# Expert 0 and the emptiest expert in turns, the plan between halves of a chunk, and the gate's bias from columns on chip

## The chip, the cores and the metric

The kernel runs on one core of a Trainium2 chip. The metric is the time of one execution on the device in microseconds (us); a profile shows one execution with every instruction of the engines: TensorE (PE), VectorE (DVE), ScalarE (ACT), GpSimd (POOL) and SyncE (SP, which here only issues transfers).

## What is computed

Two residual layers on 256 tokens of width 1024, all float32. Layer 0 is a mixer (gated delta rule beside a state-space model) and a dense SwiGLU. Layer 1 is differential attention and a mixture of experts. Before each part stands an RMS norm whose scale, shift and output gate come from `cond @ ada_w + ada_b`:

```python
mod = cond @ ada_w[layer] + ada_b[layer]          # 6 x 1024: sh1, sc1, g1, sh2, sc2, g2
x = x + g1 * mixer_or_attention(rmsnorm(x) * (1 + sc1) + sh1)
h = rmsnorm(x) * (1 + sc2) + sh2
logits = h @ router_w                             # 8 experts; the two largest of each token
for e in range(8):
    out += combine[:, e] * ((silu(h @ w1[e]) * (h @ w3[e])) @ w2[e])
x = x + g2 * out
```

The experts' weights are 8 x 33 MiB: w1 and w3 of 1024 x 2816 each, w2 of 2816 x 1024.

## The kernel before

**Weights and the ring.** Weights come from memory in tiles of 128 partitions, 1 MiB each (0.75 MiB for the third chunk), by `raw` (L105) and in `up` (L1742), all issued from SP in one queue, in order. In the expert stage there are 12 such tiles, used in a ring: a load goes out when the last use of the load twelve before it is over.

**Two forms of an expert.** Expert 0 and those with many tokens are large (128 places): `up_big` (L1656) and `down_big` split each weight tile into a rounded part `whi` (ACT, L131) and a rest `wlo` (DVE, L132) and make three products (L1674 to L1676, L1707 to L1709). The others are small (64 places): `up` (L1712 on, products L1731, L1737) and `down` (L1782) use the float32 tiles directly, in four column groups of PE. The up projection is cut into three chunks of the 2816 columns (1024, 1024, 768). Each chunk of `up_big` has two halves: first all products with w1, then a Silu, then all products with w3, then the product of both and transposes (`pth`). `tail` is a function that is called in the middle of a chunk: there the scatter of the expert before is put.

**Places and order.** `gather(r)` (L1607) brings the tokens of one expert into a buffer `xg` by products with a 0/1 matrix `Pt`; `scatter` (L1786) adds the results to `x`, with buffers `yf`, `yh`, `yl`. `plan()` (L1445) counts tokens, ranks experts 1 to 7 by count, writes the ranks' expert numbers (`idi`, L1475), their places and weights (`posS`, `combS`), and reads the numbers into registers of SP (`self.who`), which give the addresses of all weights but expert 0's; it returns `way`, which chooses among four arms of code by how many experts are large. `WAYS` gives for each the order of the ranks; rank 7 is the emptiest. In the profiled data ranks 1 and 2 are large: the order is 7, 1, 6, 5, 2, 4, 3.

Before the arms, the code runs in this order: gather 0, chunk 0 of expert 0, plan, chunks 1 and 2, gather 7, the down projection of expert 0, then the up projection of rank 7 with expert 0's scatter in its first chunk. Down of rank 7 and all else follow in the arm. The order of instructions on each engine is made by a scheduler from the order of the program and its own estimates, so that later work can stand between parts of earlier work.

**The gate's bias.** `ada_end` (L285) ends one of 24 column groups of a layer's `mod`: a sum over partitions by a product with ones. For the output gates (`which` 2 and 5, four groups each in each layer, 16 calls) it loads 256 values of `ada_b` by SP (L295), adds them to one row on POOL (L296), and makes a product that spreads the sum to all partitions (L297), which ACT copies (L298). `colA` (L231) holds all of `ada_b` on chip from the start, transposed: column 48 l + 2 j + b holds 128 values. Two of the 16 calls stand in the expert stage's beginning, four in the dense layer, the others in the mixer and the attention.

Of the kernel before, what the change touches and what calls it, by code (L numbers as in the profile page):

```python
# [9 lines left out]
F32 = mybir.dt.float32  # L10
F32R = mybir.dt.float32r
I32 = mybir.dt.int32
AF = mybir.ActivationFunctionType
ALU = mybir.AluOpType
# [3 lines left out]
P = 128  # L18
T = 256
NT = 2  # L20
D = 1024
KD = 8
# [4 lines left out]
NE = 8  # L27
# [47 lines left out]
class Trunk:  # L75
# [209 lines left out]
    def ada_end(self, l, j, s, who):  # L285
        self.mark(f"ada{l}_{j}")
        nc = self.nc
        which, o = j // 4, j % 4
        pb = self.ps(self.adatag, "gvb")
        if which in (2, 5):  # L290
            key = (l, which // 3)
            if key not in self.gates:
                self.gates[key] = (self.cp if key == (1, 1) else self.scr).tile([P, D], F32, name=self.nm("gate"), tag="gate", bufs=1)
            b = self.scr.tile([1, 256], F32, tag="adab", name=self.nm("adab"), bufs=1)
            nc.sync.dma_start(b, self.a["ada_b"][l:l + 1, 256 * j:256 * j + 256])  # L295
            nc.gpsimd.tensor_tensor(s[0:1, :], s[0:1, :], b, op=ALU.add)  # L296
            nc.tensor.matmul(pb[:, :256], who.to_broadcast([P, P]), s, start=True, stop=True)  # L297
            nc.scalar.activation(self.gates[key][:, 256 * o:256 * o + 256], pb[:, :256], AF.Copy)  # L298
            return
        for b in range(2):  # L300
            pe = nc.tensor.matmul(pb[:, b:b + 1], s[:, b * P:(b + 1) * P], who, start=True, stop=True)
        col = self.modc[(l, which)][:, 2 * o:2 * o + 2]
        b0 = l * 48 + j * 2
        nc.vector.tensor_tensor(col, pb[:, :2], self.colA[:, b0:b0 + 2], op=ALU.add)
        if which in (1, 4):
            w0 = (96 if which == 1 else 112) + l * 8 + 2 * o
            dve = nc.vector.scalar_tensor_tensor(col, col, 1.0, self.colA[:, w0:w0 + 2], op0=ALU.add, op1=ALU.mult)
            self.lastada = [pe.ins, dve.ins]
# [1089 lines left out]
    def moe(self):  # L1398
        self.mark("moe")
        nc, a, mp = self.nc, self.a, self.mp  # L1400
# [5 lines left out]
        def t(name, shape=SH):  # L1406
            return mp.tile(list(shape), F32, name=name)
# [14 lines left out]
        m1, m2, r = (t(x, (P, NT)) for x in ("m1", "m2", "r"))  # L1422
# [76 lines left out]

        self.big, self.posS, self.combS, self.who = NE, pos, comb, [0]  # L1500
        xg = self.gather(0)
        hs = []
        for c in range(len(self.CHUNKS)):
            with self.behind(self.lasts if c < 1 else ()):
                self.up_big(0, c, xg[0], hs, None)
            if c == 0:
                way = plan()
        self.big, r = 1 + self.SPLITS[-1], NE - 1
        xg1 = self.gather(r, "Pt1")
        py, steps = self.down_big(0, hs, 0, D)  # L1510
        for step in steps:
            step()
        tail, hs = partial(self.scatter, 0, py, self.places(0, xg[1]), 0, D), []
        for c in range(len(self.CHUNKS)):
            self.up(r, c, xg1[0], hs, tail if c == 0 else None, "h1")
        tc, begun, at = self.tc, (hs, xg1[1]), self.nraw

        def arm(n):
            if n + 1 == len(self.SPLITS):
                self.arm(n, begun, at)  # L1520

                with tc.If(way > n):
                    for m, caps in enumerate(self.CAPS[1:]):
                        for r in range(NE):
                            V.tensor_scalar(self.posS[:, :, r], self.posS[:, :, r], -float(self.CAPS[m][r]), None, op0=ALU.add)
                        self.experts([r for r in (0,) + self.WAYS[n] if caps[r]])
                return
# [6 lines left out]
    def arm(self, n, begun, at):  # L1534
        self.nraw, self.nsplit = at, 0
        self.big = 1 + self.SPLITS[n]
        self.experts(self.WAYS[n], begun)

    SPLITS = (2, 3, 4)
    WAYS = ((7, 1, 6, 5, 2, 4, 3), (7, 1, 6, 2, 5, 3, 4), (7, 1, 2, 6, 3, 4, 5))

# [58 lines left out]
    def mtile(self, name, shape, bufs=1, dt=F32):  # L1604
        return self.mp.tile(list(shape), dt, tag=name, name=self.nm(name), bufs=bufs)

    def gather(self, r, own="Pt"):  # L1607

        self.mark(f"gather{r}")
        V, S, PE, tile = self.nc.vector, self.nc.scalar, self.nc.tensor, self.mtile  # L1610
        big = r < self.big
        n = P if big else 64
        Pt = tile(own, (P, NT, n if own != "Pt" else P), 2 if own == "Pt" else 1)
        for tt in range(NT):
            ins = V.tensor_scalar(Pt[:, tt, :n], self.c("iota")[:, :n], self.posS[:, tt, r:r + 1], None, op0=ALU.is_equal).ins
        self.lasts = [self.xTlast, ins]
        xg = tile("xg", (P, KD, 2, P), 1, F32R)
        if not big:
            xg = xg.bitcast(F32)[:, :, 0, :]
        for k0 in range(0, KD, 4):  # L1620
            px = self.ps("ms", "px")
            for kk in range(4):
                k = k0 + kk
                for tt in range(NT):
                    PE.matmul(px[:, kk * n:kk * n + n], self.xn[:, tt, k * P:(k + 1) * P], Pt[:, tt, :n], start=(tt == 0), stop=(tt == 1))  # L1625
            f = tile("yf", (P, 512)).rearrange("p (k s) -> p k s", s=P) if big else xg[:, k0:k0 + 4]
            for kk in range(4):
                k = k0 + kk
                S.activation(f[:, kk, :n], px[:, kk * n:kk * n + n], AF.Identity, bias=self.shc[:, k:k + 1], scale=self.scc[:, k:k + 1])
            if big:  # L1630
                ks = slice(k0, k0 + 4)
                V.tensor_copy(xg[:, ks, 0, :], f)  # L1632
                V.tensor_tensor(xg[:, ks, 1, :], f, xg[:, ks, 0, :], op=ALU.subtract)
        return xg, Pt
# [202 lines left out]
```

## Time and profile before

| | us |
|---|---|
| median of 3 runs | 1382.24 (1381.57 to 1384.51) |
| profiled execution | 1378.09 |
| its span, first to last instruction | 1376.3 |
| PE busy | 1281.9 (93%) |
| DVE busy | 826.4 (60%) |
| ACT busy | 577.1 (42%) |
| transfers | 400.98 MB, mean 291 GB/s |

Busy time is that in which an engine works on an instruction; matmuls are pipelined, so a busy PE need not be at its peak. The granted clock of PE is 0.978 of full speed in the mean. Lines as L132 are lines of the kernel before; a line can be that of a helper, and `x88` counts instructions. A float32 product is two instructions.

### The profile page before, as it was taken

The numbers are of one execution on the slowest core, as the hardware profiler recorded it, in microseconds if no ns is written. First come the engines' busy times: TensorE is split into PE (matmuls) and PEld (weight loads), VectorE is DVE, ScalarE is ACT, GpSimd is POOL, SyncE is SP. The second block draws the span as 40 slices with busy tenths as digits, with TensorE's granted clock in tenths as the row PEclk, the third lists the DMA queues.
The fourth block names the chain that finished last, engine by engine and source line by source line (L and its number), as shares of the span: only waits on it lengthen the run. The fifth ranks groups of instructions, "written<-read, shape, count | busy, mean of one in ns | idle before, by whom it ended". The sixth has DMA issues, their size and how long they took to land.

```text
span 1376.3 us, 26749 instructions
## 1 busy us (share of the span) xinstructions
PE 1281.9 (93%) x10928; PEld 941.8 (68%) x10928; DVE 826.4 (60%) x1516; ACT 577.1 (42%) x990; POOL 123.6 (9%) x118
## 2 busy tenths in 40 slices
PE   3999999989999978999999999999998899999975
PEld 2777666779999978998788435786352468835334
DVE  6688767567878878965798413986020089820202
ACT  3553322455444444664778213775010168711000
POOL 3132322000000003341100000000000000000000
PEclk9799999999999999999999999999999999999998
DMA  9834334159788967821899899999999999999995
GB/s 262 268 114 132 111 106 154 62 177 325 247 270 287 293 211 252 271 96 63 334 305 399 305 380 409 405 409 356 391 409 405 408 409 406 409 397 408 408 396 208
DMA packets 196164, 400.98 MB, mean 291 GB/s; under 512 B 14797, under 2 KB 115650, under 8 KB 196034
## 3 DMA queue, kind: packets, MB, share of 16 engines
q1 hardware_dynamic: 189610, 398.00, 78.7%
q10 hardware_dynamic: 6424, 1.19, 0.5%
q8 instruction: 88, 1.44, 0.4%
q14 instruction: 42, 0.34, 0.1%
HBM read 398.11 MB, written 1.05 MB: 290 GB/s over the span
## 4 chain that ended last, share of the span: by engine, by line
PE 46%; DMA 10%; DVE 4%; issue 1%; ACT 1%; SPq 1%; POOL 0%; ACTq 0%; DVEq 0%
PE pab L1731 9%; DMA raw<-in_odd_expert_w 9%; PE py L1782 5%; PE pab L1675 4%; PE pab L1674 4%; PE pab L1676 4%; PE py L1708 2%; PE py L1709 2%; PE py L1707 2%; PE px L1625 2%; DVE wlo L132 1%; PE pqk L398 1%; PE pqk L399 1%; PE pqk L400 1%; PE pth L150 1%
## 5 line engine op out<-in xcount | busy, mean ns | idle before, releaser
L131 ACT ACTIVATE whi<-raw 128x1024 fp32r<-128x1024 f32 (+2 forms) x352 | 347.1, 1001 | 279.8 <-PE pab L399 52.3
L132 DVE TENSOR_TENSOR wlo<-raw,whi 128x1024 fp32r<-128x1024 f32 (+2 forms) x352 | 402.9, 1168 | 72.6 <-ACT whi L131 70.6
L1731 PE MATMUL pab<-raw,xg 128*32 128x512 f32 (+1 forms) x1920 | 194.2, 524 | 10.5 <-DMA raw<-in_odd_expert_w 10.5
L1731 PEld LDWEIGHTS pab<-raw,xg 128*32 128x32 f32 x1920 | 58.2, 109 | 118.8 <-issue 77.5
L1751 DVE TENSOR_TENSOR hb<-hb,pab 128x256 f32<-128x256 f32 (+1 forms) x35 | 12.4, 364 | 171.0 <-ACT hb L1750 170.5
L1675 PE MATMUL pab<-wlo,xg 128*128 128x512 f32 (+1 forms) x288 | 110.3, 383 | 3.6 <-DVE wlo L132 3.4
L1676 PE MATMUL pab<-whi,xg 128*128 128x512 f32 (+1 forms) x288 | 106.4, 377 | 0.0
L398 PE MATMUL pab<-hT,whi 128*128 128x256 f32 x352 | 101.9, 290 | 0.0
L399 PE MATMUL pab<-hT,whi 128*128 128x256 f32 x352 | 100.3, 285 | 0.1
L400 PE MATMUL pab<-hT,wlo 128*128 128x256 f32 x352 | 99.9, 284 | 0.0
L1782 PE MATMUL py<-raw,hTe 128*32 128x256 f32 (+1 forms) x1760 | 83.7, 343 | 10.7 <-DMA raw<-in_odd_expert_w 8.6
L282 DVE SCALAR_TENSOR_TENSOR adas<-raw,condr,adas 128x256 f32<-128x256 f32 x175 | 86.4, 499 | 3.1
L1674 PE MATMUL pab<-whi,xg 128*128 128x512 f32 (+1 forms) x288 | 84.4, 379 | 3.6 <-DVE xg L1632 1.9
L1782 PEld LDWEIGHTS py<-raw,hTe 128*32 128x32 f32 x1760 | 53.4, 112 | 38.0 <-DMA raw<-in_odd_expert_w 12.8
L1802 DVE TENSOR_TENSOR yf<-py,gate 32x256 f32<-32x256 f32 (+1 forms) x48 | 18.0, 374 | 102.3 <-PE py L1782 101.3
L1750 ACT ACTIVATE hb<-pab 128x256 f32<-128x256 f32 (+1 forms) x35 | 11.5, 338 | 155.8 <-PE pab L1731 155.1
L399 PEld LDWEIGHTS pab<-hT,whi 128*128 128x128 f32 x352 | 68.0, 193 | 0.8 <-DVE hT L388 0.5
L398 PEld LDWEIGHTS pab<-hT,whi 128*128 128x128 f32 x352 | 68.1, 193 | 0.3
L400 PEld LDWEIGHTS pab<-hT,wlo 128*128 128x128 f32 x352 | 67.9, 193 | 0.1
L1675 PEld LDWEIGHTS pab<-wlo,xg 128*128 128x128 f32 x288 | 54.3, 189 | 19.4 <-DVE wlo L132 6.3
L1676 PEld LDWEIGHTS pab<-whi,xg 128*128 128x128 f32 x288 | 54.4, 189 | 10.0
L1674 PEld LDWEIGHTS pab<-whi,xg 128*128 128x128 f32 x288 | 51.0, 189 | 13.7 <-ACT whi L131 2.2
(465 smaller groups left out, 2504.4 us busy)
## 6 DMA issues: line engine op xcount, KB each, us to landing
raw<-in_odd_expert_w SPq DMA_DIRECT2D x215, 1024.0 KB
raw<-in_ada_w SPq DMA_DIRECT2D x48, 1024.0 KB
raw<-in_odd_expert_w SPq DMA_DIRECT2D x64, 768.0 KB
raw<-in_even_ffn_w SPq DMA_DIRECT2D x33, 1024.0 KB
raw<-in_odd_w_qkv SPq DMA_DIRECT2D x12, 1024.0 KB
raw<-in_even_w_in SPq DMA_DIRECT2D x10, 1024.0 KB
raw<-in_even_w_out SPq DMA_DIRECT2D x4, 1024.0 KB
raw<-in_odd_w_out SPq DMA_DIRECT2D x4, 1024.0 KB
```

The source lines that it names most:

```text
L131: act = nc.scalar.activation(hs, src, AF.Copy)
L132: dve = nc.vector.tensor_tensor(l, src, hs, op=ALU.subtract)
L282: nc.vector.scalar_tensor_tensor(s, w[:, k, :], self.condr[:, k, 0:1], s, op0=ALU.mult, op1=ALU.add)
L398: nc.tensor.matmul(out, wh[:, o:o + P], hT[:, k, 0, :], start=(k == 0), stop=False)
L399: nc.tensor.matmul(out, wh[:, o:o + P], hT[:, k, 1, :], start=False, stop=False)
L400: nc.tensor.matmul(out, wl[:, o:o + P], hT[:, k, 0, :], start=False, stop=(k == kd - 1))
L1625: PE.matmul(px[:, kk * n:kk * n + n], self.xn[:, tt, k * P:(k + 1) * P], Pt[:, tt, :n], start=(tt == 0), stop=(tt == 1))
L1674: PE.matmul(p[:, :m], xg[:, k, 0, :], wh[:, s], start=(k == 0), stop=False)
L1675: PE.matmul(p[:, :m], xg[:, k, 0, :], wl[:, s], start=False, stop=False)
L1676: PE.matmul(p[:, :m], xg[:, k, 1, :], wh[:, s], start=False, stop=(k == KD - 1))
L1731: PE.matmul(pu[t][32 * g:32 * g + 32], xg[:, k, 32 * t:32 * t + 32], v[:, :, g * n:(g + 1) * n], start=(k == 0 and (t == 0 or n > P)), sto ...
L1782: PE.matmul(py[32 * g:32 * g + 32, t], hs[f][t], v[:, i, g * n:(g + 1) * n], start=(f == 0 and t == 0), stop=(f == NF - 1 and t == 1))
```

## The change

Four edits. The bias of the gate is added by two more products into the same accumulator, a column of `colA` spread over 128 columns against the identity; the load, the small buffer and the POOL addition go. The plan is called as `tail` of expert 0's first chunk, between its two halves. The up projection of rank 7 stands between the chunks of expert 0: expert 0 chunk 0, chunk 1, gather 7 (its output in the buffer `yh` instead of `xg`), rank 7 chunk 0, expert 0 chunk 2, rank 7 chunk 1, expert 0 down, rank 7 chunk 2 with expert 0's scatter. `WAYS` has rank 6 second, before rank 1.

```diff
-            b = self.scr.tile([1, 256], F32, tag="adab", name=self.nm("adab"), bufs=1)
-            nc.sync.dma_start(b, self.a["ada_b"][l:l + 1, 256 * j:256 * j + 256])
-            nc.gpsimd.tensor_tensor(s[0:1, :], s[0:1, :], b, op=ALU.add)
-            nc.tensor.matmul(pb[:, :256], who.to_broadcast([P, P]), s, start=True, stop=True)
+            nc.tensor.matmul(pb[:, :256], who.to_broadcast([P, P]), s, start=True, stop=False)
+            for b in range(2):
+                row = l * 48 + j * 2 + b
+                nc.tensor.matmul(pb[:, b * P:(b + 1) * P], self.colA[:, row:row + 1].to_broadcast([P, P]), self.ident,
+                                 start=False, stop=(b == 1))
...
-        hs = []
-        for c in range(len(self.CHUNKS)):
-            with self.behind(self.lasts if c < 1 else ()):
-                self.up_big(0, c, xg[0], hs, None)
-            if c == 0:
-                way = plan()
-        self.big, r = 1 + self.SPLITS[-1], NE - 1
-        xg1 = self.gather(r, "Pt1")
-        py, steps = self.down_big(0, hs, 0, D)
+        h0, hs, got = [], [], []
+        with self.behind(self.lasts):
+            self.up_big(0, 0, xg[0], h0, lambda: got.append(plan()))
+        way, r, big = got[0], NE - 1, 1 + self.SPLITS[-1]
+        self.up_big(0, 1, xg[0], h0, None)
+        self.big = big
+        xg1 = self.gather(r, "Pt1", "yh")
+        self.up(r, 0, xg1[0], hs, None, "h1")
+        self.up_big(0, 2, xg[0], h0, None)
+        self.up(r, 1, xg1[0], hs, None, "h1")
+        py, steps = self.down_big(0, h0, 0, D)
         for step in steps:
             step()
-        tail, hs = partial(self.scatter, 0, py, self.places(0, xg[1]), 0, D), []
-        for c in range(len(self.CHUNKS)):
-            self.up(r, c, xg1[0], hs, tail if c == 0 else None, "h1")
+        self.up(r, 2, xg1[0], hs, partial(self.scatter, 0, py, self.places(0, xg[1]), 0, D), "h1")
...
-    WAYS = ((7, 1, 6, 5, 2, 4, 3), (7, 1, 6, 2, 5, 3, 4), (7, 1, 2, 6, 3, 4, 5))
+    WAYS = ((7, 6, 1, 5, 2, 4, 3), (7, 6, 1, 5, 2, 3, 4), (7, 6, 1, 2, 3, 4, 5))
...
-    def gather(self, r, own="Pt"):
+    def gather(self, r, own="Pt", at="xg"):
...
-        xg = tile("xg", (P, KD, 2, P), 1, F32R)
-        if not big:
-            xg = xg.bitcast(F32)[:, :, 0, :]
+        if at == "xg":
+            xg = tile("xg", (P, KD, 2, P), 1, F32R)
+            if not big:
+                xg = xg.bitcast(F32)[:, :, 0, :]
+        else:
+            xg = tile(at, (P, 512), 1, F32R).bitcast(F32).rearrange("p (k s) -> p k s", s=n)
```

## Rows read from the trace of the kernel before

**Rows 1.** The page's slices (40 equal ones): busy tenths of PE, GB/s.

```profile
PE   3999999989999978999999999999998899999975
GB/s 262 268 114 132 111 106 154 62 177 325 247 270 287 293 211 252 271 96 63 334 305 399 305 380 409 405 409 356 391 409 405 408 409 406 409 397 408 408 396 208
```

**Rows 2.** Windows: us of each engine and instructions, PE clock, DMA share, GB/s.

```profile
640.00:680.00 40.00, 36.75 (x291) 33.43 (x292) 24.97 (x67) 22.50 (x51) 4.69 (x7) 0.96 0.69 258
680.00:700.00 20.00, 20.00 (x88) 16.11 (x87) 17.21 (x16) 16.82 (x18) 0.52 (x1) 1.00 0.96 346
700.00:720.00 20.00, 20.00 (x95) 16.39 (x94) 19.11 (x36) 15.19 (x18) 0.00 (x0) 1.00 0.89 296
720.00:740.00 20.00, 20.00 (x115) 17.43 (x114) 19.68 (x32) 17.24 (x22) 0.00 (x0) 1.00 1.02 395
740.00:760.00 20.00, 20.00 (x111) 15.83 (x109) 15.54 (x17) 15.24 (x23) 0.00 (x0) 1.00 0.95 369
760.00:780.00 20.00, 20.00 (x90) 10.34 (x90) 9.13 (x8) 7.42 (x7) 0.00 (x0) 1.00 0.71 261
780.00:800.00 20.00, 20.00 (x145) 7.54 (x144) 4.84 (x8) 2.03 (x4) 0.00 (x0) 1.00 1.03 408
800.00:820.00 20.00, 20.00 (x246) 8.53 (x250) 2.26 (x4) 1.96 (x4) 0.00 (x0) 1.00 0.98 363
```

**Rows 3.** Waits of SP's queue from 640 to 700 us: total, times, longest.

```profile
SPq L110 <- DVE wlo L132: 63.5, 11, 38.3
SPq L295 <- PE plg L1393: 11.0, 1, 11.0
```

**Rows 4.** Timeline of SP, loads one by one: start, duration in us.

```profile
685.19 0.37 SPq L110 DMA_DIRECT2D raw<-in_odd_expert_w  x1
...
720.45 0.37 SPq L110 DMA_DIRECT2D raw<-in_odd_expert_w  x1
724.03 0.37 SPq L110 DMA_DIRECT2D raw<-in_odd_expert_w  x1
...
736.59 0.67 SPq L1742 DMA_DIRECT2D raw<-in_odd_expert_w  x1
```

**Rows 5.** Groups by line from 640 us on: busy us, mean ns, idle before.

```profile
L1731 PE MATMUL pab<-raw,xg 128*32 128x512 f32 (+1 forms) x1920 | 194.2, 524 | 10.5 <-DMA raw<-in_odd_expert_w 10.5
L1625 PE MATMUL px<-Pt,xn 128*128 128x64 f32 (+1 forms) x256 | 30.8, 275 | 2.1 <-DMA raw<-in_odd_expert_w 1.2 <-DVE Pt L1615 0.9
```

**Rows 6.** Timeline of ACT, PE and DVE around the first two chunks: start, us.

```profile
687.05 1.09 ACT L1680 ACTIVATE hb<-pab 128x512 f32<-128x512 f32 x2
...
701.74 1.03 PE L150 MATMUL pth<-cst,hb 128*128 128x128 f32 x8
708.22 0.51 PE L1458 MATMUL pcnt<-A,ones 128*128 128x8 f32 x4
...
717.04 0.15 DVE L1475 CAST idi<-ids 1x7 int32<-1x7 f32 x1
...
723.18 0.60 PE L150 MATMUL pth<-cst,hb 128*128 128x128 f32 x4
```

**Rows 7.** Windows near the ends of the later large experts, columns as in rows 2.

```profile
930.00:940.00 10.00, 10.00 (x45) 8.09 (x45) 7.22 (x9) 8.26 (x12) 0.00 (x0) 1.00 0.93 354
950.00:960.00 10.00, 10.00 (x69) 4.85 (x67) 3.51 (x5) 0.97 (x2) 0.00 (x0) 1.00 0.90 325
960.00:970.00 10.00, 10.00 (x84) 3.48 (x80) 3.42 (x5) 0.63 (x1) 0.00 (x0) 1.00 0.97 346
...
1210.00:1220.00 10.00, 10.00 (x74) 3.51 (x75) 4.09 (x6) 1.26 (x2) 0.00 (x0) 1.00 1.00 387
1220.00:1230.00 10.00, 9.87 (x86) 2.79 (x84) 2.25 (x4) 0.77 (x2) 0.00 (x0) 1.00 1.02 398
```

**Rows 8.** A window of the dense layer, columns as in rows 2.

```profile
340.00:360.00 20.00, 20.00 (x145) 18.92 (x144) 15.64 (x24) 8.58 (x14) 0.72 (x1) 1.00 0.70 225
```

**Rows 9.** The chain of waits in order of time, one piece near its end.

```profile
1341.77 14.75 DMA raw<-in_odd_expert_w
```

## The prediction

> **What bounds the kernel now.** I read the slices first, then the expert stage in windows, then the queue that issues loads, then durations.
>
> The slices [rows 1] show two regimes. Up to about 640 us PE is busy nine tenths or more while the transfers run at 60 to 330 GB/s; from about 850 us they stand at 400 to 409 GB/s until the last slice, and that is the ceiling: 408 GB/s, or 2.57 us for one load of 1 MiB (every expert weight tile is 1 MiB, those of the third chunk 0.75). The chain of waits near the end runs through a transfer, not through an engine [rows 9]. So a change pays in the expert stage only by the transfer time that it saves before about 820 us or in later holes, and before 640 us by what PE gains or loses.
>
> The windows [rows 2] show the hole: from 680 to 820 us the transfers fall short of 408 GB/s by 62, 112, 13, 39, 147, 0 and 45 GB/s, each over 20 us, together 418 x 20 / 408 = 20.5 us of transfer time, with PE busy throughout. The cause is in the queue's waits [rows 3]: a load waits until a tile is free. There are 12 tiles in a ring, so load i goes out when load i-12 is used up. A large expert uses one up in 12 products of 20 / 88 = 0.227 us [rows 2], 2.73 us, slower than 2.57; the emptiest expert (64 places) in 16 instructions of 0.101 us [rows 5], 1.62 us. With the ring full, 35 loads of the slow kind in a row hold the transfers back.
>
> **The change part by part.** Count in loads of 1 MiB moved. At 720 us the kernel before has moved 3 (issued before 640) + (40 x 258 + 20 x 346 + 20 x 296) / 1048.6 = 25.1 [rows 2]; at 820 us 25.1 + 20 x (395 + 369 + 261 + 408 + 363) / 1048.6 = 59.4.
>
> *Order of expert 0 and the emptiest.* Nothing is added to or taken from PE: the same products in another order. The 28 loads whose tiles the first two chunks free are out by 718.5 us (load 28 goes at 720.45 [rows 4]). They now hold 24 whole loads and four of 0.75, 27 MiB, in place of 26. Load 28 then needs the first tile of the emptiest expert: end of the second chunk at 724.5 [rows 6], its gather of 32 instructions x 0.12 = 3.8 [rows 5], one tile 1.6: about 730. At 730 us the transfers stand at 27, where before they stood at 25.1 + 3.8 = 28.9: for a moment the change is behind. From there tiles come free every 1.6 us, then every 2.0 for the short third chunk, then 1.6 again, and the backlog covers the down projection; the transfers have no reason to stop, and at 820 us they stand at 27 + 90 / 2.57 = 62.0. Ahead by 2.6 loads, **-6.8 us**. If the gather is worked into the second chunk, so that load 28 goes 5 us sooner, up to -11.8; if the small products are mixed into the large ones as the kernel before mixes them after 750 us (the 147 GB/s hole), down to -3.
>
> *Turns 7, 6, 1, 5 in place of 7, 1, 6, 5.* A lead is kept only while the ring has room. The first large expert after expert 0 loses (54 + 83 + 62) x 10 / 408 = 4.9 us when the ring fills near its end, the second, which starts after two small ones with its lead used up, (21 + 10) x 10 / 408 = 0.8 [rows 7]. In the new turns the first starts after the emptiest and another small one, like the second now; the second starts after one small one. A small expert's up part uses 384 x 0.101 = 39 us of PE for 22 loads that take 57, so it works off any lead. I expect losses of about 0.8 and 3: **-2 us** (bounds 0 and -5). Without the new turns the 2.6 loads would be lost in that first hole.
>
> *Plan between halves.* The plan's some 35 small VectorE operations stay; they move. But the emptiest expert's loads need its number in registers of SyncE, and nothing passes it in that in-order queue. Before, they were issued at 736.59 [rows 4], 19.5 us after the number was written at 717.04 [rows 6]: that cover goes. Now the first of them is load 16, whose tile is free at 685.19 [rows 4]. The plan was reached after the first chunk's transposes (701.74) and had the number 14.5 us after their end at about 702.5; reached after the Silu of the first half (687.05 + 1.09 [rows 6]) it has it at 702 to 703. While the queue stands, the ring drains: loads 0 to 15 are in by about 688. To have 27 at 730 the queue must go on by 730 - 11 x 2.57 = 701.7; each us later costs one. With a register read or two on top I take **+2 us** (bounds 0 and +5; the rival below is the tail). Queued behind the wait are all weight loads; PE does not notice, it has 16 loads of work until 724.
>
> The Trainium skill, page "DMA: Bandwidth & Descriptors", section "Latency and other measured facts", gives a floor of about 600 ns for a tensor_load. If each of the seven register reads cost that, the queue would be held an estimated 4.2 us more and the sum would come out near no change. The rows allow less than that in one place: between the loads of 720.45 (0.37 long) and 724.03 [rows 4], soon after the number was written, there are 3.2 us, part of which is the wait for a tile.
>
> *Bias of the gate.* Each of 16 calls loses a 1 KB transfer, a wait of SyncE for it and a GpSimd addition, and gains two products of 128 columns, two instructions each at 0.12 us (a gather's price [rows 5]): 0.48 us of PE, 7.7 for all. Four fall into the dense layer, where PE is busy 20.00 of 20 us [rows 8]: +1.9 in full. Ten stand in the mixer and attention weaves and two in the expert stage, where PE is at nine tenths or more [rows 1] but other chains have a part; I count half of their 5.8 and give back 0.8 for the addition that no longer stands before the gate's product: **+4 us** (bounds 1 and 7.7). The longest wait that goes is SyncE's 11.0 us behind the router's product [rows 3], ending at about 663. The three loads behind it may move up, but the loads from the thirteenth on wait for tiles that the first chunk frees, so I count nothing; at most 5 us.
>
> *Sum.* -6.8 - 2 + 2 + 4 = -2.8 us. The profiled execution took 1378.09 us (span 1376.3, 1.8 around it), so 1375.3 for a like one; the median of the three shown is 4.15 higher, 1382.24, and I forecast **1379.4** on that scale.
>
> **Rivals.**
> *The queue stands still for the expert's number (slower).* Place: SyncE between loads 15 and 16. If VectorE, busy 19.11 of 20 us from 700 [rows 2], gives the plan's chain no earlier place than now, the number comes at 717 and the queue is 15.3 us late: -6.8 - 2 + 4 + 15.3 = +10.5, 1392.7. It decides from 701.7 + 4.8 = 706.5 on (level), and is clear of level at 709. For it: the chain from count to number took 8.8 us for some ten operations [rows 6], strung between splits. Against: the plan is reached 14 us earlier. The register price of the skill's page would push this way by an estimated 4 us.
> *The bias eats the gain (no change).* All 16 calls pay in full, 7.7, and the turns give nothing: -6.8 + 7.7 + 2 = +2.9; with half of either, 0. Some 1382 to 1385. For it: PE at nine tenths almost everywhere. Against: the idle of PE before 640 us lies just in the weaves.
> *No pause at 722 (more gained).* The number is early, the gather runs inside the second chunk, the bias costs 2: -11.8 - 2 + 2 = -11.8, 1370 to 1373. For it: the gather no longer needs the buffer of expert 0's input, so only its places hold it.
> *The lead is not kept (the change does not do what it says).* The ring fills in the next large expert all the same: 4.8 + 2 lost, leaving the +4 and +2, 1386 to 1388. Against: one more small expert comes before it.
>
> **How the numbers follow.** Forecast case (1375 to 1381.5): 45%. More gained: 18%. No change: 17%. Queue stands: 13%. Lead lost: 7%. About 0.2% (2.8 us) is what a measurement can tell here. Below 1379.5 lie the second case and seven tenths of the first: 0.50. Within 2.8 us of before: the rest of the first and two thirds of the third: 0.25. Above: 0.25. For 8 in 10 the range reaches into the gaining case and into the standing queue: 1369 to 1391; the forecast case alone is 1375 to 1381.5.
>
> **What would show it.** Right: in windows after the change, 720 to 730 us below 300 GB/s, then 400 or more without a break to 820; the second large expert's end losing more than the first; the last transfer some 7 us earlier against the start of the experts' products, and that start 3 to 4 us later than 674. Wrong: SyncE idle after load 15 beyond 707 (the number), transfers under 400 between 740 and 800 (mixed products), or a start of the experts' products that has not moved (the bias is hidden).

## The result, and the profile after

The change is slower: 1386.59 us in the median of 12 runs against 1379.70 for the kernel before beside it, ratio 1.0053 [1.0035, 1.0070], or +7.3 us; on the scale of the forecast, 1.0053 x 1382.24 = 1389.6, at the far end of its range and on the other side of before. The profiled execution took 1384.23 us (span 1382.5) against 1378.09 (1376.3), +6.1. The slices, after (they answer [rows 1]):

```profile
PE   3999999989999988999999999998999999999975
GB/s 256 272 122 123 123 102 144 62 131 329 243 273 301 292 230 236 260 123 9 316 333 225 409 405 407 407 406 409 406 409 399 407 409 406 406 377 407 408 397 224
```

The ceiling of 408 GB/s is reached from about 760 us on, but the slices from 590 to 690 us (123, 9, 316) together move less than before (96, 63, 334). The same windows as [rows 2], then two of [rows 7] and the one of [rows 8] (us of PE, PEld, DVE, ACT, POOL with instructions; PE clock, DMA share, GB/s):

```profile
640.00:680.00 40.00, 37.71 (x306) 35.20 (x305) 22.27 (x63) 23.30 (x57) 4.30 (x6) 0.88 0.46 165
680.00:700.00 20.00, 20.00 (x98) 17.26 (x97) 16.74 (x50) 13.61 (x22) 0.00 (x0) 0.90 0.96 360
700.00:720.00 20.00, 20.00 (x92) 16.28 (x91) 18.96 (x21) 16.48 (x19) 0.00 (x0) 1.00 0.92 339
720.00:740.00 20.00, 20.00 (x107) 17.02 (x107) 16.87 (x19) 14.85 (x20) 0.00 (x0) 1.00 0.66 234
740.00:760.00 20.00, 20.00 (x171) 9.60 (x170) 4.04 (x6) 6.29 (x14) 0.00 (x0) 1.00 0.80 254
760.00:780.00 20.00, 20.00 (x121) 9.21 (x119) 5.75 (x8) 4.38 (x7) 0.00 (x0) 1.00 1.03 410
...
950.00:960.00 10.00, 9.58 (x40) 6.93 (x39) 10.00 (x12) 6.72 (x8) 0.00 (x0) 1.00 1.03 409
...
1220.00:1230.00 10.00, 10.00 (x75) 3.44 (x78) 5.49 (x8) 1.26 (x2) 0.00 (x0) 1.00 0.98 355
...
340.00:360.00 20.00, 20.00 (x143) 18.88 (x143) 13.25 (x19) 8.24 (x12) 0.00 (x0) 1.00 0.68 230
```

The pause is there (720 to 760), nothing stops behind it until 1190, the first large expert's hole is gone and the second's is there. So the shape is the forecast one, though the 400 GB/s without a break begin 73 us after expert 0's first product, where the forecast had 56. What isn't as forecast is the start: that product stands at 686.6 us, not at 674.2, and the forecast gave 3 to 4 us for that (PE's timeline of after, then of before):

```profile
686.55 0.48 PE L1678 MATMUL pab<-whi,xg 128*128 128x512 f32 x1
...
674.17 0.51 PE L1674 MATMUL pab<-whi,xg 128*128 128x512 f32 x1 [1.90 <-DVE xg L1632]
```

The chain still ends in transfers (its pieces near the end answer to [rows 9]):

```profile
1321.30 16.19 DMA raw<-in_odd_expert_w
1342.29 12.82 DMA raw<-in_odd_expert_w
```

The queue's longest waits (answering [rows 3]): the wait behind the router's product is still there, though the bias load that showed it is gone; now a weight load has it.

```profile
SPq L110 <- DVE wlo L132: 59.9, 9, 38.3
SPq L1746 <- DVE wlo L132: 13.8, 7, 2.7
SPq L110 <- PE plg L1394: 11.8, 1, 11.8
```

The number of the emptiest expert and the loads (answering [rows 4, 6]; timeline of PE, DVE and SP, start and duration; last, the line of SP's reads of the numbers, with the shortest, median and longest in ns and the first and last start):

```profile
686.18 0.51 PE L1459 MATMUL pcnt<-A,ones 128*128 128x8 f32 x4
693.26 0.15 DVE L1476 CAST idi<-ids 1x7 int32<-1x7 f32 x1
697.63 0.68 SPq L1746 DMA_DIRECT2D raw<-in_odd_expert_w  x1
...
740.46 0.37 SPq L110 DMA_DIRECT2D raw<-in_odd_expert_w  x1
...
L1494 SPq TENSOR_LOAD <-idi x7: 263/268/464, 695.5 to 811.1; - x7
```

The count stands ahead of expert 0's first product, and the number is there 7 us after that start. The first load that needs it goes 2.86 us after the load before (694.77), the pace of the large tiles: no such wait as the rival's 15 us. Of the seven reads of numbers into SP's registers one, of 0.46 us, stands ahead of that load (695.55); the other six stand at 809 to 811 us.

Because the starts differ, the expert stages are compared by what is still to be transferred so many us after expert 0's first product, in MiB ahead of the kernel before, its lead (5-us windows summed, interpolated; one MiB is 2.57 us). The kernels below the first row are those of the experiments.

| kernel | first product at, us | +46 us | +66 | +146 | +186 | +326 | +626 |
|---|---|---|---|---|---|---|---|
| after | 686.6 | 1.4 | -3.0 | 0.8 | 0.7 | 2.9 | 1.9 |
| e2: after, old bias | 676.4 | 1.3 | -3.4 | 0.9 | 0.0 | 2.1 | 0.6 |
| e3: e2, old turns | 674.3 | 1.3 | -3.5 | 0.9 | 0.9 | -1.9 | -1.8 |
| f1: before, new turns | 675.8 | -0.1 | -0.5 | 0.4 | 0.4 | 2.6 | 1.5 |
| g1: e2, mended order | 675.7 | 1.3 | -0.2 | 1.8 | 1.8 | 4.0 | 2.5 |

The row of after is the balance of its profile: 12.4 us late at the start, 1.9 MiB or 4.9 us regained by 626 us later, 1.3 in the tail, which leaves it 6.2 us late. Each row is one execution.

### The profile page after: what moved, and what is told of

It is laid out like the page before. It is cut to its first block, busy times and chain, and to the rows that moved or that the text cites. A ratio compares the mean times of both kernels' runs of the same rounds, so it can differ in the third digit from the quotient of the medians.

```text
span 1382.5 us, 26813 instructions
## 1 busy us (share of the span) xinstructions
PE 1293.3 (94%) x10992; PEld 956.5 (69%) x10992; DVE 825.5 (60%) x1516; ACT 576.9 (42%) x990; POOL 104.6 (8%) x102
## 4 chain that ended last, share of the span: by engine, by line
PE 63%; DMA 6%; DVE 5%; issue 2%; ACT 1%; POOL 0%; SPq 0%; ACTq 0%; DVEq 0%; POOLq 0%
PE pab L1735 11%; PE py L1786 6%; DMA raw<-in_odd_expert_w 5%; PE pab L1679 4%; PE pab L1678 4%; PE pab L1680 4%; PE pab L399 3%; PE pab L400 3%; PE pab L401 3%; PE px L1629 3%; PE py L1712 2%; PE py L1713 2%; PE py L1711 2%; DVE wlo L132 2%; PE facc L407 1%
## 5 line engine op out<-in xcount | busy, mean ns | idle before, releaser
L1735 PE MATMUL pab<-raw,xg 128*32 128x512 f32 (+1 forms) x1536 | 149.1, 524 | 6.0 <-DMA raw<-in_odd_expert_w 6.0
L1735 PEld LDWEIGHTS pab<-raw,xg 128*32 128x32 f32 x1536 | 45.9, 110 | 89.7 <-issue 63.4
L1755 DVE TENSOR_TENSOR hb<-hb,pab 128x256 f32<-128x256 f32 (+1 forms) x35 | 12.3, 362 | 158.0 <-ACT hb L1754 157.7
L1754 ACT ACTIVATE hb<-pab 128x256 f32<-128x256 f32 (+1 forms) x35 | 11.4, 337 | 157.9 <-PE pab L1735 157.3
```

What stands on the lines that cost most here:

```text
L1735: PE.matmul(pu[t][32 * g:32 * g + 32], xg[:, k, 32 * t:32 * t + 32], v[:, :, g * n:(g + 1) * n], start=(k == 0 and (t == 0 or n > P)), sto ...
```

## Experiments

Times are medians; each ratio is to runs of the kernel before on the same chip (medians 1378.4 to 1379.8). A difference of two kernels is worked out from their ratios, its half width (the +-) as the root of the sum of squares of the two.

**One edit at a time.** e1 is the kernel before with the first hunk of the change alone. e2 is the changed kernel with that hunk taken back; e3 is e2 with the old turns; e4 is e2 with the gather of the emptiest expert inside expert 0's second chunk:

```diff
-    WAYS = ((7, 6, 1, 5, 2, 4, 3), (7, 6, 1, 5, 2, 3, 4), (7, 6, 1, 2, 3, 4, 5))
+    WAYS = ((7, 1, 6, 5, 2, 4, 3), (7, 1, 6, 2, 5, 3, 4), (7, 1, 2, 6, 3, 4, 5))     # e3
...
-        self.up_big(0, 1, xg[0], h0, None)
         self.big = big
-        xg1 = self.gather(r, "Pt1", "yh")
+        self.up_big(0, 1, xg[0], h0, lambda: got.append(self.gather(r, "Pt1", "yh")))     # e4
+        xg1 = got[1]
```

> The kernel before with only the gate's bias changed. Theory A (the bias edit costs the time ahead of the experts, directly by its 64 added instructions and by another order of the mixer's work): the experts' first product moves from 674.2 to 682 to 685 us and the whole is slower than before by 6 to 10 us (ratio 1.0045 to 1.007). Rival B (the new order in the expert stage costs it): within 3 us of before, first product within 3 us of 674. Rival C (the 64 instructions at their price alone): +7.7 us at most ahead of and in the experts, with the mixer's end (last out projection product of layer 0, 297 us before) at most 2 us later.

Measured 1390.57, 1.0087 [1.0062, 1.0113]: +12.0 us, three times the forecast's term and more than theory A's 6 to 10; expert 0's first product stands at 688.2 us in its profile.

> The changed kernel with the bias as before (load and GpSimd addition): only plan, order and turns changed. Theory A: everything ahead of the experts as before, first product at 674 to 676 us, and 3 to 8 us faster than before (the forecast's -6.8 - 2 with a longer pause at 727 us than forecast). Rival B: slower than before by 0 to 5 us, since the pause of the transfers at 729 to 758 us (14.7 us short in the changed kernel) is not won back.

Measured 1378.31, 0.9992 [0.9977, 1.0008]: level. So the bias costs 8.4 +- 3.2 us in the change (forecast 4), and the other three edits together bring nothing that can be told from zero, where theory A had 3 to 8 us.

> As e2_no_bias but with the turns 7, 1, 6, 5 of before. If the new turns keep the lead, this is 2 to 5 us slower than e2_no_bias, with the transfers short of 408 GB/s again near the end of the first large expert after expert 0. If the turns give nothing, equal within 2 us.

Measured 1382.56, 1.0031 [1.0014, 1.0047]: the turns are worth 5.4 +- 3.1 us here; the new order without them costs 4.3. Its lead is lost between 880 and 1000 us; there e3 loses 13.2 us of transfers, e2 0.5 and the kernel before 6.0 (shortfall: the transfer time lost against 408 GB/s, summed over 10-us windows; two windows of e3):

```profile
880.00:900.00 20.00, 20.00 (x92) 16.30 (x92) 18.07 (x18) 16.25 (x18) 0.00 (x0) 1.00 0.92 310
930.00:960.00 30.00, 30.00 (x149) 23.58 (x148) 21.78 (x20) 19.64 (x25) 0.00 (x0) 1.00 0.98 366
```

> As e2_no_bias, but the emptiest expert's gather is called between the halves of expert 0's second chunk instead of after it. If load 28 and those behind it wait for the gather and the first small products (the pause at 729 to 758 us), the pause shrinks by the 8 us between the second chunk's end and the first small product, and the whole is 3 to 7 us faster than e2_no_bias. If the pause is set by something else (tiles used up slowly by the mix of large and small products), equal within 2 us.

Measured 1377.16, 0.9989 [0.9971, 1.0008], the same as e2. The early gather spreads the pause (710 to 750 us at 309, 214, 215 and 337 GB/s) and hardly shortens it: 13.7 us short of 408 in those 40 us, 14.7 in e2. The profiled execution of e4 (1382.43 us) lies 5 us above its median.

**Where the bias costs.** f2 and f3 are e2 with the new bias in some of the calls, f4 without any bias, f1 the kernel before with the new turns alone (the diff line above, reversed):

```diff
+            if (l, which) == (0, 2):     # f2, the mixer's four calls; f3 has !=, the other twelve
+                ... two bias products
+            else:
+                ... load and addition
```

> The new order, plan and turns; bias from the columns on chip only in the four calls of the mixer, by load and addition in the other twelve. Theory (order): what the bias costs beyond its products comes from the mixer, where the scheduler arranges everything behind the first call in another way, so that PE waits 2 us for a state vector near 215 us and runs 5 to 10 us at a lower clock: 1378.3 + 5 = 1383 to 1384. Rival (price): each call costs the same wherever it stands, 8.3 / 16 = 0.52 us: 1378.3 + 2.1 = 1380.4.

Measured 1390.30, 1.0063 [1.0037, 1.0088]: 9.8 +- 4.1 us over e2, more than the 5 of theory (order) and far from the 2.1 of theory (price).

> The complement: bias from the columns in the twelve calls of the dense layer, the attention and the expert stage, by load and addition in the four of the mixer, whose order stays as before. Theory (order): twelve calls pay at most their products, 1.9 in the dense layer and 1 to 2 behind it: 1378.3 + 3 = 1381 to 1382. Rival (price): 12 x 0.52 = 6.2, 1384.5. A third: the two calls of the expert stage, whose products stand between those of the first gather, cost 3 us by themselves: then 1384 with the first gather to first expert product 3 us longer than without the bias.

Measured 1377.50, 0.9981 [0.9962, 1.0000]: -1.5 +- 3.4 against e2, below all three theories. As far as these two can tell, the whole loss lies in the four calls of the mixer.

> The new order, plan and turns; the bias of the gates left out altogether (no load, no addition, no products). Nothing is added to PE. Theory (order): taking the load and the addition away alone makes the scheduler arrange the mixer in another way, and that is what costs: 1381 to 1383, with PE waiting for the state vector near 215 us as with the products. Rival (price): the cost is the products; without them the gates are 0.8 us earlier and nothing is lost: 1377 to 1378.5.

This one answers only in part: without the bias the router picks other experts (three large ones behind expert 0 in place of two), so its time (1398.03, 1.0129) can't be set beside the others. Its mixer can: the dense layer began at 301.9 us, earlier than in any kernel here (305.8 in the kernel before, 308.4 in e2, 314.7 in f2). So the theory that any other order in the mixer costs falls, though the order of VectorE, ScalarE and GpSimd is another than before here too.

> The kernel before with the new turns alone (rank 6 before rank 1); expert 0, plan and bias as before. The turns took 4.2 us off when the new order of expert 0 stood under them (1382.6 to 1378.3). Theory: they keep the first large expert from filling the ring, whatever stands ahead of it, and are worth about the same alone: 1375 to 1377 against 1379.4 of before, and the loss of transfers near 930 to 960 us becomes less than 2 us. Rival: they only keep a lead that the new order makes, and there is none here: 1379 to 1380.

Measured 1374.69, 0.9966 [0.9949, 0.9983]: -4.7 us. The turns stand by themselves, and this edit alone beats the whole change by 12 us.

What happens in the mixer is seen where after, e1 and f2 are alike and differ from the rest. Windows of before, then of after:

```profile
210.00:215.00 5.00, 5.00 (x47) 2.91 (x47) 4.15 (x10) 1.14 (x3) 1.76 (x1) 1.00 1.03 364
215.00:220.00 5.00, 4.37 (x70) 3.11 (x66) 4.46 (x8) 0.89 (x2) 1.27 (x1) 1.00 0.26 87
220.00:225.00 5.00, 4.55 (x42) 2.71 (x42) 4.86 (x12) 0.00 (x0) 0.64 (x1) 1.00 0.59 198
```

```profile
210.00:215.00 5.00, 4.47 (x56) 2.82 (x56) 1.45 (x5) 1.53 (x3) 0.00 (x0) 1.00 0.55 208
215.00:220.00 5.00, 3.23 (x19) 2.07 (x23) 4.93 (x10) 0.00 (x0) 1.23 (x1) 0.64 0.00 0
220.00:225.00 5.00, 5.00 (x30) 2.56 (x23) 4.00 (x11) 0.38 (x1) 1.59 (x2) 0.68 0.00 0
```

In after VectorE is busy 1.45 of 5 us from 210 to 215, PE is idle behind it, and then runs at a mean clock of 0.64 and 0.68 of 2.4 GHz, so partly at 1.2. The timeline of after (ACT, DVE and PE; in brackets the idle time before and what ended it) names the cause:

```profile
214.07 0.63 ACT L131 ACTIVATE whi<-raw 128x512 fp32r<-128x512 f32 x1 [1.75 <-DMA raw<-in_even_glu_w]
214.74 0.69 DVE L132 TENSOR_TENSOR wlo<-raw,whi 128x512 fp32r<-128x512 f32 x1 [1.55 <-ACT whi L131]
215.34 0.68 DVE L1109 TENSOR_TENSOR s5a<-bu,cos 128x512 f32<-128x512 f32 x1
215.94 0.68 DVE L1110 TENSOR_TENSOR s5b<-bu,sin 128x512 f32<-128x512 f32 x1
211.99 1.12 PE L1101 MATMUL bu<-uT,wb 32*128 32x256 f32 x4
216.77 2.04 PE L1101 MATMUL bu<-uT,wb 32*128 32x256 f32 x4 [2.11 <-DVE s5b L1110]
```

VectorE stands in its queue at a weight split (`wlo`) that waits for ScalarE's part, and that for a load, and the state products `s5a`, `s5b`, whose input `bu` was there since about 213, stand behind it; PE waits 2.11 us for them, and its next four products take 2.04 us where four of the same form took 1.12 at 212 us. In the order of VectorE's instructions, after, e1 and f2 have two weight splits ahead of this pair, the kernel before and e2 one. The scheduler makes that order anew from its own estimates when something ahead of it changes. PE's wait for `s5b` is 2.1, 2.0 and 2.9 us in after, e1 and f2. f4 has the two splits too, and PE waits 0.4 us there, since the second load was in earlier; the other twelve kernels have no such wait.

The wait is the smaller part of the cost. From the first state product (`bu`) to the dense layer after, e1 and f2 take 144.8, 146.4 and 145.4 us, the other thirteen kernels 135.3 to 137.5. PE's mean clock in that stretch is 0.93 in the three and 0.96 to 0.99 in the others: by that, an estimated 6 of the 9 us are the clock and some 2 idle time. The windows above hold 3.4 us of the clock's part; the rest is spread over the stretch and its cause is not shown.

**The same products elsewhere, and the order mended.** g3 is the changed kernel with the bias products ahead of the sum's product; that puts one split ahead of the pair again. g1 is e2 with expert 0's down projection directly behind its third chunk and its scatter among the emptiest expert's products, for which the scatter's rounded part needs another buffer. g2 and g4 are f1 with one edit more (bias as in f3; plan between the halves).

```diff
+            for b in range(2):                                                        # g3
+                ... bias product, start=(b == 0), stop=False
+            nc.tensor.matmul(pb[:, :256], who.to_broadcast([P, P]), s, start=False, stop=True)
...
         self.up_big(0, 2, xg[0], h0, None)                                            # g1
-        self.up(r, 1, xg1[0], hs, None, "h1")
         py, steps = self.down_big(0, h0, 0, D)
         for step in steps:
             step()
-        self.up(r, 2, xg1[0], hs, partial(self.scatter, 0, py, self.places(0, xg[1]), 0, D), "h1")
+        self.up(r, 1, xg1[0], hs, partial(self.scatter, 0, py, self.places(0, xg[1]), 0, D, True), "h1")
+        self.up(r, 2, xg1[0], hs, None, "h1")     # True: yh lies in the buffer xg
```

> The changed kernel with the same 32 bias products, but ahead of the product that spreads the sum, not behind it. In the order of instructions the 7th and 8th last pair of state products (s5a, s5b) then have one weight split (wlo) ahead of them on VectorE again, as before the change, in place of two. Theory (order of the mixer): the wait for s5b near 215 us and the clock of 0.5 to 0.7 behind it go, and nearly all of the 8 to 10 us: 1377 to 1380. Rival (the products themselves, wherever they stand): no change, 1386.

Measured 1377.59, 0.9983 [0.9963, 1.0003]: 9.7 +- 3.7 us less than after, with the same 32 products, and level with e2 (-1.2 +- 3.5), which has none of them. PE's wait for `s5b` is gone and the clock is whole here:

```profile
215.00:220.00 5.00, 3.83 (x49) 2.64 (x48) 5.00 (x9) 0.39 (x1) 1.26 (x1) 1.00 0.24 75
220.00:225.00 5.00, 5.00 (x48) 3.09 (x51) 4.86 (x12) 0.00 (x0) 1.22 (x1) 1.00 0.47 166
```

> The new order with bias by load and addition (1378.3 so far), but expert 0's down projection directly behind its third chunk, then the emptiest expert's second chunk with expert 0's scatter in it, then its third chunk; the scatter's rounded part goes to the buffer of expert 0's input so that it can start before the emptiest expert is done. Theory: the order loses at the end of the block, where the scatter stands last, PE waits for ScalarE, the clock falls to 0.50 from 830 to 840 us and the ring runs out (2.5 us of transfers at 835 to 850); with the scatter among products that hole goes: 1375 to 1376.5, transfers at 400 or more from 740 to 1040. Rival: what the order loses is the pause at 720 to 740 alone; then nothing changes, 1378 to 1379.

Measured 1371.19, 0.9942 [0.9921, 0.9962]: 6.9 +- 3.5 less than e2, more than expected, because two holes closed. Windows of e2, then of g1:

```profile
720.00:730.00 10.00, 9.67 (x64) 8.27 (x63) 7.69 (x10) 6.24 (x11) 0.00 (x0) 1.00 0.37 141
730.00:740.00 10.00, 10.00 (x88) 3.96 (x91) 0.96 (x1) 2.02 (x5) 0.00 (x0) 1.00 0.48 137
820.00:830.00 10.00, 6.90 (x51) 3.47 (x43) 6.11 (x14) 2.36 (x6) 0.00 (x0) 0.87 1.03 408
830.00:840.00 10.00, 10.00 (x66) 7.99 (x70) 0.00 (x0) 2.58 (x8) 0.00 (x0) 0.50 1.00 400
840.00:850.00 10.00, 10.00 (x174) 5.32 (x170) 0.00 (x0) 0.38 (x1) 0.00 (x0) 0.95 0.88 314
```

```profile
720.00:730.00 10.00, 9.67 (x66) 8.34 (x65) 7.69 (x10) 5.80 (x13) 0.00 (x0) 1.00 0.73 241
730.00:740.00 10.00, 10.00 (x91) 3.55 (x93) 0.96 (x1) 1.70 (x5) 0.00 (x0) 1.00 1.00 363
820.00:830.00 10.00, 8.29 (x103) 6.05 (x97) 1.58 (x7) 3.03 (x10) 0.00 (x0) 1.00 1.03 407
830.00:840.00 10.00, 10.00 (x186) 5.76 (x178) 0.00 (x0) 1.17 (x4) 0.00 (x0) 1.00 1.02 408
840.00:850.00 10.00, 10.00 (x181) 5.72 (x176) 0.80 (x2) 0.00 (x0) 0.00 (x0) 1.00 1.03 408
```

At 820 e2's scatter stands last in the block, ahead of the branch into an arm, with no products to stand between its steps: PE is busy 6.90 of 10 us, then runs ten at 0.50 (1.2 GHz), tiles come free too slowly, and the transfers thin to 314 GB/s once the ring is full. This place doesn't cost in every execution: after, f3 and g3 have the scatter there and a clock of 0.50 to 0.51 for ten us too, and their lead from +146 to +186 us holds (0.8 to 0.7, 0.7 to 0.7, 0.3 to 0.4 MiB), while e2, f2 and e4 lose 0.9, 1.1 and 3.1; and h1, with g1's order, has 0.55 for ten us and loses 0.4.

The pause at 720 the waits of SP's queue tell, from 700 to 745 us (total, times, longest); e2, then g1:

```profile
SPq L110 <- PE pab L1734: 17.4, 4, 13.6
```

```profile
SPq L110 <- PE pab L1734: 11.2, 7, 3.4
```

In e2 one load of expert 0's third chunk waits 13.6 us for a tile of the emptiest expert, whose products begin at 731.9 us, though the third chunk's own first products, drawn in around the gather, free tiles from 724 on: the queue is in order and each load is bound to one tile. In g1 three loads of the down projection (724.60, 727.53, 729.27) go ahead of it into such tiles.

> The kernel before with the new turns (1374.7) and the bias from columns in the twelve calls behind the mixer. Those twelve changed the time by -0.8 us under the new order (1378.3 to 1377.5, within what can be told), though the experts' first product stood 5 us later in that one profile. Theory (the twelve cost nothing): 1374 to 1375. Rival (they cost their products, and the two of the expert stage delay the first expert): 1378 to 1380.

Measured 1377.36, 0.9988 [0.9966, 1.0009]: +3.0 +- 3.8 on f1, not told apart.

> The kernel before with the new turns (1374.7) and the plan between the halves of expert 0's first chunk, all else in the old order. Here nothing waits for the early number, so the plan itself can only cost: some 35 VectorE operations between splits. Theory (the plan is free, the +3.6 us between this and the new order belong to the order's end): 1374 to 1375.5. Rival (the plan delays splits of the second half, PE waits): 1377 to 1379.

Measured 1377.79, 0.9989 [0.9968, 1.0011]: +3.2 +- 3.8 on f1, not told apart either; its lead in MiB is f1's at +46 to +326 us (0.1, -0.2, 0.5, 0.5, 2.6), so where 3 us should come from isn't seen.

**All four edits, mended, and the turns once more.** h1 is g1 with the bias as in g3; h2 is g1 with the old turns.

```diff
-                nc.gpsimd.tensor_tensor(s[0:1, :], s[0:1, :], b, op=ALU.add)          # h1: load and addition go,
+                ... bias products ahead of the sum's product, as g3
...
-    WAYS = ((7, 6, 1, 5, 2, 4, 3), ...
+    WAYS = ((7, 1, 6, 5, 2, 4, 3), ...                                                # h2
```

> All four edits, mended: expert 0's scatter among the emptiest expert's products, the bias products of all 16 gates ahead of the product that spreads the sum. With the bias by load and addition this stood at 1371.2. Theory (once the mixer's order is left as it was, the 32 products cost little, since under the unmended order they stood at 1377.6 against 1378.3): 1370 to 1372.5. Rival (the twelve later calls cost their products, 0.48 us each and more before the first expert; 2.7 us showed under the old order of expert 0, within what can be told): 1374 to 1377.

Measured 1373.43, 0.9959 [0.9934, 0.9984]: 5.7 us faster than before, +2.3 +- 4.5 on g1. Whether the new bias costs 0 or 3 us once the mixer's order is left alone stays open: the twelve later calls give -1.5 (f3 to e2) and +3.0 (g2 to f1), all sixteen -1.2 (g3 to e2) and +2.3 (h1 to g1), each +- 3.4 to 4.5.

> The mended order of expert 0 (1371.2) with the old turns (rank 1 before rank 6). The turns were worth 4.2 us under the unmended order and 4.7 us on the kernel before. Theory (they act after 880 us and don't depend on what stands ahead): 1375 to 1376.5, with a hole of 4 to 6 us of transfers between 880 and 990. Rival (the mended order carries its lead by itself): 1371 to 1373.

Measured 1380.26, 1.0010 [0.9992, 1.0028]: without the turns the mended order's lead of 1.8 MiB is lost as well, 12.3 us of shortfall from 880 to 1000. The turns are worth 9.4 +- 3.8 there, more than theory or rival allowed. g1 has the lowest median of all, but against f1, the turns alone, it is -3.3 +- 3.7: that the mended order is worth anything beyond the turns is not shown.

## Why the prediction was wrong

Term by term, from the ratios: forecast, then measured.

| term | forecast | measured |
|---|---|---|
| order of expert 0 and plan, under the new turns | -4.8 | +3.6 +- 3.2 (e2 to f1) |
| new turns | -2 | -4.7 [-7.0, -2.3] (f1) |
| gate's bias | +4 | +8.4 +- 3.2 (after to e2) |
| sum | -2.8 | +7.3 [+4.8, +9.7] |

**The order failed (its -6.8), at "the transfers have no reason to stop".** Up to the pause it went as worked out: load 28 goes 53.9 us after the first product, 728 on the time axis of the kernel before, where "about 730" stood, and 56 us after that product the balance is -1.6 MiB in after and -1.7 in e2 where the forecast had -1.9. Ten us later the forecast's own numbers give -1.7, but after has -3.0 and e2 -3.4: the sum let the transfers go at 408 GB/s from the moment load 28 was issued. From 740 to 760 us after moved 186 and 322 GB/s, 7.5 us of transfers short of 408. Third-chunk products and the gather stood ahead of the small ones until 743.3 us, so the next four loads went 2.9 us apart (740.46 to 752.16). In e2 the small ones came sooner, but the pause between two loads was 14 us (719.52 to 733.87), and the transfers took until 741 us to come back to 390 GB/s. The forecast named mixed products as a lower bound, "down to -3". From there to +146 us the gain is nearly the forecast one, so of the 2.6 loads after had 0.8 and e2 0.9, and g1 1.8; f1 without the new order had 0.4.

The scatter of expert 0, which [rows 2] hides among products at 800 to 820, became the last thing before a branch; in e2 its idle time and low clock emptied the lead, 0.9 MiB at +146 us to 0.0 at +186. I had counted the scatter's products and not what stood between them. In after's own profile the lead survived this place, so how much of the +3.6 us it makes is not shown.

**The bias failed as a price list.** In the dense layer the price was right: four calls made 190.1 us of products 191.9, +1.8 where +1.9 stood. "Half of their 5.8" for the weaves was wrong in kind: the four calls of the mixer cost 9.8 +- 4.1 us by another order of instructions on VectorE, and with that order undone (g3) all sixteen cost nothing that can be told. The upper bound of 7.7 was all products in full, and no bound covered a reordering. After's own start, 12.4 us late, is made of 5.4 up to the dense layer, 1.8 in the dense layer, 2.0 in the attention and 3.2 between the router's and the first expert's product. The 5.4 are one execution against one: the mixer lost 9.5 us by the stretch above, and after had reached its first state product 4.2 us earlier than before (166.4 against 170.6). Of the 3.2 a part is the clock, at 0.50 to 0.60 from 670 to 685 us: that stretch takes 14.6 us in after, 12.2, 10.5 and 12.2 in g3, h1 and f3 with the same products in it, 11.4 before.

**The turns were right in place and small in size.** Shortfalls of 0.8 and 3 us were forecast for the two large experts; after shows 0.5 (880 to 1000) and 2.9 (1190 to 1250). But the loss that they avoid was not 4.9: it was 6.0 in the kernel before, since [rows 7] left out some windows of that hole, and with the old turns it grew to 13.2 under the new order.

**The plan's term of +2 was nothing in the queue, in part by luck.** The number was there at 693.26, ahead of load 15 (694.77), because the scheduler put the count ahead of expert 0's first product; the forecast had placed the plan behind the first half's Silu. Loads 16 and 24 go 11.1 and 34.3 us after the first product, 11.0 and 34.7 in the kernel before, so the queue lost nothing and the rival of the standing queue falls. The Trainium skill, page "DMA: Bandwidth & Descriptors", section "Latency and other measured facts", gives a floor of about 600 ns for a tensor_load, an estimated 4.2 us for seven. The trace has them shorter, one of 0.46 us and six of 0.26 to 0.29, and only the first ahead of the loads; the measurement decides. The forecast looked for the reads in the wrong place: in the kernel before the first stands at 735.50 us (0.47 long), not between the loads of 720.45 and 724.03.

Of the rivals, "the lead is not kept" (1386 to 1388) lies nearest by the number, but after kept a lead (2.9 MiB at +326 us); it is what e3 and h2 show without the turns. "The bias eats the gain" named the right edit, but by its price and only up to 1385.

## What to carry over

An edit that a scheduler sees is priced twice: by its instructions where it stands, and by the order that it makes of all that follows; compare the written order of each engine before and after, and look for an instruction that waits for a load with others queued behind it. A step that is moved to the end of a block loses the work that covered its gaps, so ask what it stands among, not only how long it is. Time each edit by itself: here the smallest of the four, alone, did as well as anything that could be told from it. When the ring of buffers bounds the transfers, follow each load to the tile it is bound to.

## What the runs showed of the hardware

- After a short idle time PE's clock fell for several us: 3.23 us busy in 5 was followed by a clock of 0.68 in the next 5 with PE fully busy (after, 220 us), and 6.90 in 10 by 0.50 for all of the next 10 (e2, 830 us). Yet 3.83 in 5 (g3, 215 us) was followed by 1.00. Where the clock fell, a wait of 2.1 us was joined by some 3.4 us lost to the clock (an estimate: 0.36 and 0.32 of two windows of 5 us in after).
- The same order of instructions on VectorE, ScalarE and GpSimd put the dense layer's start anywhere from 305.8 (before) to 310.3 us (f3) in the ten kernels whose mixer is unchanged, 307.6 in the mean. Single profiles differ by 4.5 us without a cause in the code, which is why differences here rest on medians of up to 12 runs. With the harmful order (after, e1, f2) it is 311.2 to 316.4, 314.1 in the mean; g3 and h1 have 305.1 and 304.3.
- A read of a number from on-chip memory into a register of SP took 0.46 us by itself and 0.26 to 0.29 us in a row of six (after, 695.55 and 809 to 811 us).
